# Attention on one core: the exponential of 15 of 256 score units computed on VectorE and GpSimd

## The chip, the cores and the metric

The kernel runs on one core of a Trainium2 chip. The metric is the device time of one execution in microseconds (us). TensorE (PE in the profile) multiplies matrices, ScalarE (ACT) evaluates functions such as exp, VectorE (DVE) and GpSimd (POOL) do elementwise work, and SyncE (SP) issues most of the transfers. SBUF is the on-chip working memory and PSUM the memory that TensorE writes its results to. All of these run in parallel; each takes its own instructions in order, and waits on the others through semaphores.

## The reference

```python
def reference(q, k, v):                       # each (8, 8, 512, 64), float32
    scale = 1.0 / np.sqrt(q.shape[-1])
    scores = np.einsum('bhqd,bhkd->bhqk', q, k) * scale
    scores = scores - scores.max(axis=-1, keepdims=True)
    attn = np.exp(scores)
    attn = attn / attn.sum(axis=-1, keepdims=True)
    return np.einsum('bhqk,bhkd->bhqd', attn, v)
```

There are 64 heads of 512 queries and 512 keys, each with 64 features. The inputs are standard normal numbers, and the kernel takes the exponential of the scaled scores without subtracting the maximum.

## The kernel before, in words

Heads are taken in 32 pairs g. For a pair, q, k and v are loaded as float32 (`load`, L66, on SP's queue), six pairs ahead. GpSimd casts q and k of both heads into one float16 tile (`cast_qk`, L86 to L95, tag qk, four buffers, three pairs ahead) and v into a tile with a column of ones beside it (`cast_v`, L97 to L103, five tiles vp used in turn). TensorE transposes q and k of the pair in eight 128x128 matmuls into PSUM, and VectorE copies the result to SBUF (`transpose`, L108 to L120, tile tqk).

The score work is cut into 256 units (g, c, h): 128 keys (chunk c of 4) by 512 queries of head h. One matmul of 512 columns makes a unit's scores, keys on the partitions (`scores`, L152 to L161). Three units share one PSUM tile st of 128x1536; there are two such tiles. One ScalarE instruction takes the exponential of all three into the float16 tile pt (`softmax`, L163 to L166, eight buffers). The list `sizes` (L146) cuts the units into groups of 1, 1, 2, then 3 throughout, then 2 and 1.

For each head, `attend` (L201 to L208) multiplies the exponentials with v: 16 matmuls of 128 queries by 65 columns over the four key chunks (`weigh`, L170 to L181), into a PSUM tile o. The 65th column is the sum of the exponentials, by the column of ones. `normalise` (L183 to L193) takes its reciprocal (L187, tile rcp) and multiplies (L188, tile osb) on VectorE, both reading o from PSUM. `save` stores both heads of a pair on SP's queue (L196).

The transposes and the o tiles share one small PSUM ring: `aux` (L105, tag ps_x) has two buffers, so a tile can be written only when the tile two before it has been read out.

The order of everything is written out by hand in the main loop (L270 to L298), once per group j: `softmax(j)`, then `scores(j + 1)`, then whatever falls due for the units of group j - 1. With the first unit of a pair g come `cast_qk(g + 3)`, `cast_v(g + 2)` and the loads of pairs g + 6 (q, k) and g + 5 (v). With its third unit a transpose of g + 2 is put in the list `work`, and with the last key chunk of a head that head's `attend`. A group lets pieces of `work` go while its credit lasts:

```python
            credit = min(credit + 0.42 * n, 2.0)
            while work and (credit >= 1.0 or j > len(sizes) - 6):
                f, *a = work.popleft()
                f(*a)
                credit -= 1.0
```

So one or two such pieces are issued per group of three units. Each engine's queue follows this order: on TensorE the scores of a group stand ahead of its pieces of work; on VectorE there is a copy or a normalisation for each piece; on GpSimd there are three casts per pair; on SP there are three loads per pair and one store. The first pair (L218 to L268) and the last head (`close`, L210) have code of their own.

Of the kernel before, what the change touches and what calls it, by code (L numbers as in the profile page):

```python
# [8 lines left out]

FP32 = mybir.dt.float32  # L10
FP16 = mybir.dt.float16

EXP = mybir.ActivationFunctionType.Exp
AluOp = mybir.AluOpType


@with_exitstack
def kernel(
# [4 lines left out]
    v: bass.AP,  # L23
    out: bass.AP,
):

    nc = tc.nc
    B, H, S, D = q.shape  # L30
    P = 128
    NI = S // P
    assert NI == 4 and D == 64 and S == 512
    scale = float(D) ** -0.5
    W = D + 1

    n_pairs = (B * H) // 2
    ppb = H // 2
    UPP = 2 * NI
    last = n_pairs - 1  # L40
    units = []
    for g in range(n_pairs):
        if g in (0, last):
            first = NI - 1 if g == 0 else 0
            units += [(g, (first + c) % NI, h) for h in range(2) for c in range(NI)]
        else:
            units += [(g, c, h) for c in range(NI) for h in range(2)]
    n_units = len(units)
    G = 3
    NV = 5  # L50
    AHEAD = 6
# [4 lines left out]
    ppool = ctx.enter_context(tc.tile_pool(name="att_p", bufs=8))  # L56
# [9 lines left out]
    def load(g, names="qkv"):  # L66
        if g >= n_pairs:
            return
        for nm in names:
            r = lpool.tile([P, 2, NI * D], FP32, tag=f"{nm}32", name=f"{nm}32_{g}")  # L70
            nc.sync.dma_start(out=r, in_=rows(dict(q=q, k=k, v=v)[nm], g))
            raw[g, nm] = r

    def load_head(h, nm, eng):
        if ("head", h) not in raw:
            raw["head", h] = cpool.tile([P, 2 * NI, D], FP32, name=f"raw_0_{h}")
        lo = NI * "kq".index(nm)
        eng.dma_start(
            out=raw["head", h][:, lo : lo + NI].rearrange("p (o i) d -> p o (i d)", o=1),
            in_=rows(dict(q=q, k=k)[nm], 0, h, h + 1),  # L80
        )

    vps = [cpool.tile([P, 2, NI, W], FP16, name=f"vp{n}") for n in range(NV)]
    halves, tqk, turned = {}, {}, {}

    def cast_qk(g):  # L86
        if g >= n_pairs:
            return
        qk = xpool.tile([P, 2, NI, P], FP16, tag="qk", name=f"qk_{g}")
        for n in range(2):  # L90
            nc.gpsimd.tensor_copy(  # L91
                out=qk[:, n].rearrange("p i (h d) -> p i h d", d=D),
                in_=raw[g, "qk"[n]].rearrange("p h (i d) -> p i h d", d=D),
            )
        halves[g] = qk  # L95
# [9 lines left out]
    def aux(shape, dt, name):  # L105
        return pspool.tile(shape, dt, tag="ps_x", bufs=2, name=name)

    def transpose(g, parts=(0, 1)):  # L108
        if g >= n_pairs:
            return  # L110
        if g not in turned:
            turned[g] = xpool.tile([P, 2, S], FP16, tag="tqk", name=f"tqk_{g}")
            for h in range(2):
                tqk[g, h] = [turned[g][D * h : D * (h + 1), n] for n in range(2)]
        lo, hi = parts[0], parts[-1] + 1
        ps = aux([P, hi - lo, NI, P], FP16, f"tps_{g}_{lo}")
        for n in parts:
# [7 lines left out]
    def open_cast(h, eng, lo, hi):  # L125


        if ("x", h) not in raw:
            raw["x", h] = cpool.tile([P, N, D], FP16, name=f"x_0_{h}")
            f = cpool.tile([D, NI + 1, P], FP16, name=f"t_0_{h}")  # L130
            r = cpool.tile([D, FIRST, P], FP16, name=f"r_0_{h}")
            raw["t", h] = f, r
            keys = [r[:, c] for c in range(FIRST)] + [f[:, 0]]
            tqk[0, h] = (f[:, 1:].rearrange("d n p -> d (n p)"), keys)
        eng(out=raw["x", h][:, lo:hi], in_=raw["head", h][:, lo:hi])  # L135
# [9 lines left out]

    sizes = [1, 1, 2] + [G] * ((n_units - 7) // G) + [2, 1]  # L146
    assert sum(sizes) == n_units
    firsts = [sum(sizes[:j]) for j in range(len(sizes))]
    where = {units[f + x]: (j, x) for j, (f, s) in enumerate(zip(firsts, sizes)) for x in range(s)}
    st, pt = {}, {}  # L150

    def scores(j):  # L152
        if j >= len(sizes):
            return
        if j not in st:
            st[j] = pspool.tile([P, G, S], FP32, tag="ps_st", bufs=2, name=f"st_{j}")
        for x in range(sizes[j]):
# [2 lines left out]
            key = tk[c] if g == 0 else tk[:, c * P : (c + 1) * P]  # L160
            nc.tensor.matmul(st[j][:, x, :], key, tq, start=True, stop=True)  # L161

    def softmax(j):  # L163
        n = sizes[j]
        pt[j] = ppool.tile([P, G, S], FP16, tag="pt", name=f"pt_{j}")
        nc.scalar.activation(out=pt[j][:, 0:n], in_=st[j][:, 0:n], func=EXP, scale=scale)  # L166
# [2 lines left out]

    def weigh(g, h, o, chunks, blocks=range(NI)):  # L170
        for c in chunks:
            j, x = where[g, c, h]
            for i in blocks:
                nc.tensor.matmul(  # L174
                    o[:, i, :],
                    pt[j][:, x, i * P : (i + 1) * P],
                    vps[g % NV][:, h, c, :],
                    start=(c == 0 and i == blocks[0]),
                    stop=(c == NI - 1),
                    skip_group_check=True,  # L180
                )  # L181
# [36 lines left out]
    with tc.manual_schedule():  # L218
        load_head(0, "q", nc.sync)
        load_head(0, "k", nc.scalar)  # L220
        load_head(1, "q", nc.sync)
        load_head(1, "k", nc.scalar)
        blank = cpool.tile([P, P], FP16, name="blank")
        nc.vector.memset(blank, 0.0)
        small = cpool.tile([P, 1], FP32, name="small")
        nc.vector.memset(small, 0.0)  # L226
        nc.scalar.activation(out=small, in_=small, func=EXP, scale=scale)  # L227
        ident16 = cpool.tile([P, P], FP16, name="ident16")
        make_identity(nc, ident16)
        load(1, "qk")  # L230
        load(0, "v")
        for g in range(2, AHEAD):
            load(g, "qk")
            load(g - 1, "v")
        for n in range(NV):
            nc.vector.memset(vps[n][:, :, :, D:W], 1.0)
        def busy(tile, n):
            for _ in range(n):
                nc.tensor.matmul(tile[:, G - 1, 0:P], blank, blank, start=True, stop=True)  # L239

        busy(pspool.tile([P, G, S], FP32, tag="ps_st", bufs=2, name="warm"), 24)
        A, V, Y = nc.scalar.copy, nc.vector.tensor_copy, nc.gpsimd.tensor_copy
        open_cast(0, V, 3, 6)
        open_cast(0, A, 6, 8)
        open_cast(0, A, 0, 3)
        open_cast(1, Y, 0, 3)
        a1, a2 = (aux([D, N, P], FP16, f"open_{n}") for n in range(2))
        a3 = pspool.tile([D, N, P], FP16, tag="ps_st", bufs=2, name="open_2")
        open_turn(0, 3, 6, a1)
        open_turn(0, 6, 8, a2)  # L250
        open_turn(0, 0, 3, a3)
        open_copy(0, V, 3, 6, a1)
        open_copy(0, A, 6, 8, a2)
        open_cast(1, V, 3, 8)
        open_copy(0, V, 0, 3, a3)
        st[0] = pspool.tile([P, G, S], FP32, tag="ps_st", bufs=2, name="st_0")
        busy(st[0], 4)
        scores(0)
        scores(1)
        b1, b2 = (aux([D, N, P], FP16, f"open_{n + 3}") for n in range(2))  # L260
        open_turn(1, 3, 8, b1)
        open_turn(1, 0, 3, b2)
        open_copy(1, V, 3, 8, b1)
        open_copy(1, V, 0, 3, b2)
        cast_qk(1)
        cast_v(0)
        cast_qk(2)
        cast_v(1)  # L268

        work = deque()  # L270
        credit = 0.0
        for j, n in enumerate(sizes[:-1]):
            softmax(j)
            if j > 0:
                scores(j + 1)
                if j == 2:
                    transpose(1, (0,))
                    transpose(1, (1,))
                for u in range(firsts[j - 1], firsts[j - 1] + sizes[j - 1]):
                    g, c, h = units[u]  # L280
                    r = u % UPP
                    if r == 0:
                        cast_qk(g + 3)
                        cast_v(g + 2)
                        load(g + AHEAD, "qk")
                        load(g + AHEAD - 1, "v")
                    if r == (5 if g == 0 else 2) and g + 2 < n_pairs:
                        work.append((transpose, g + 2))
                    if c == (FIRST - 1 if g == 0 else NI - 1):
                        work.append((attend, g, h))  # L290
            credit = min(credit + 0.42 * n, 2.0)
            while work and (credit >= 1.0 or j > len(sizes) - 6):
                f, *a = work.popleft()
                f(*a)
                credit -= 1.0
        while work:
            f, *a = work.popleft()
            f(*a)  # L298
        close()
# [30 lines left out]
```

The softmax here doesn't subtract the row's maximum and nothing guards it: scores larger than these inputs give would overflow.

## Time and profile before

| | us |
|---|---|
| median of the 3 runs shown | 129.53 |
| lowest and highest of them | 126.96, 129.73 |
| the profiled execution | 126.88 |
| its span, first to last instruction | 125.1 |
| ScalarE busy in the span | 117.5 |
| TensorE matmuls busy | 107.2 |
| VectorE busy | 60.7 |
| GpSimd busy | 58.9 |

The profile is of one execution. Its page gives the busy time of each engine, the span in 40 slices, the DMA queues, the chain of work that ended last, and groups of instructions: line, engine and operation, output tile <- input tiles with shapes, count | busy us, mean ns of one | idle time of the engine just before them, and what ended most of it. Timelines list start, length, engine, line and instruction. TensorE's granted clock was 0.999 of full speed. The DMA queues moved 33.81 MB at a mean of 270 GB/s.

### The profile page before, as it was taken

Reading aid. Unit: us, or ns where it says so; the run is one execution under the profiler, and the core shown is the slowest. Engines: PE = TensorE matmul, PEld = TensorE weight load, DVE = VectorE, ACT = ScalarE, POOL = GpSimd, SP = SyncE. Lnnn points to the kernel's source line nnn. Section 1 sums busy time; section 2 is a strip of 40 time slices with the busy share of each in tenths; the row PEclk is TensorE's granted clock in tenths of the full one; section 3 lists DMA queues with packets and bytes.
Section 4 is the critical chain, followed back from the end, with each engine's and each line's share of the span. In section 5 each row is a group of like instructions: output and inputs, shape, how many; then the busy total and the mean of one; then the engine's idle time right before and its main releaser. Section 6 shows DMA issues by size and latency. Waiting matters only on the chain.

```text
span 125.1 us, 3986 instructions
## 1 busy us (share of the span) xinstructions
PE 107.2 (86%) x1572; PEld 63.9 (51%) x1572; DVE 60.7 (49%) x173; ACT 117.5 (94%) x93; POOL 58.9 (47%) x101
## 2 busy tenths in 40 slices
PE   6999979889997987999798798979979898997780
PEld 6636536455464454565455265545536455554450
DVE  0344536553653745445454554645546563553450
ACT  4499999999999999999999999999999999999970
POOL 2188878576565173376347523644753753000000
PEclk9999999999999999999999999999999999999999
DMA  3999999999997699999789878989999974222222
GB/s 111 290 354 350 349 350 370 365 372 375 359 355 220 177 298 332 368 341 330 219 252 364 284 246 212 368 278 289 375 302 282 350 262 147 89 84 86 89 78 89
DMA packets 34882, 33.81 MB, mean 270 GB/s; under 512 B 2096, under 2 KB 34864, under 8 KB 34864
## 3 DMA queue, kind: packets, MB, share of 16 engines
q1 hardware_dynamic: 34576, 33.30, 82.0%
q8 instruction: 12, 0.20, 0.7%
q10 hardware_dynamic: 288, 0.26, 0.6%
q14 instruction: 6, 0.05, 0.1%
HBM read 25.17 MB, written 8.39 MB: 268 GB/s over the span
## 4 chain that ended last, share of the span: by engine, by line
ACT 74%; issue 16%; PE 4%; DMA 2%; DVE 1%
ACT pt L166 74%; DMA raw<-in_k_dram 2%; PE open L139 1%; PE st L161 1%; PE o_last L174 1%; PE o L174 0%; PE st L239 0%; DVE osb L188 0%; DVE x L135 0%; DVE rcp L187 0%
## 5 line engine op out<-in xcount | busy, mean ns | idle before, releaser
L166 ACT ACTIVATE pt<-st 128x1536 f16<-128x1536 f32 (+2 forms) x88 | 115.1, 1597 | 1.0 <-PE st L161 1.0
L161 PE MATMUL st<-tqk 64*128 64x512 f16 x248 | 49.6, 380 | 13.1 <-ACT pt L166 11.5
L174 PEld LDWEIGHTS <-pt 128*128 128x128 f16 x1024 | 33.8, 98 | 18.0 <-issue 16.2
L174 PE MATMUL o<-vp,pt 128*128 128x65 f16 x1008 | 38.4, 194 | 0.0
L91 POOL CAST qk<-q 128x512 f16<-128x512 f32 x31 | 19.1, 616 | 27.4 <-DMA q<-in_q_dram 19.6
L187 DVE RECIPROCAL rcp<-o 128x4 f32<-128x4 f32 x63 | 11.3, 180 | 38.8 <-PE o L174 38.8
L120 DVE COPY tqk<-tps 128x1024 f16<-128x1024 f16 (+1 forms) x32 | 21.5, 675 | 15.4 <-PE tps L119 15.4
L188 DVE TENSOR_TENSOR osb<-o,rcp 128x256 f32<-128x256 f32 x63 | 26.7, 425 | 2.2
L100 POOL CAST vp<-v 128x512 f16<-128x512 f32 x32 | 19.8, 619 | 10.6 <-DMA v<-in_v_dram 6.4
L161 PEld LDWEIGHTS <-tqk 64*128 64x128 f16 x248 | 11.6, 93 | 23.4 <-issue 14.8
L91 POOL CAST qk<-k 128x512 f16<-128x512 f32 x31 | 19.1, 616 | 5.6 <-DMA k<-in_k_dram 4.7
L119 PEld LDWEIGHTS <-qk 128*128 128x128 f16 x248 | 13.9, 98 | 13.1 <-issue 9.3
L119 PE MATMUL tps<-ident,qk 128*128 128x128 f16 x248 | 19.2, 220 | 0.0
L239 PE MATMUL warm<-blank 128*128 128x128 f16 x24 | 2.7, 310 | 1.0 <-DVE small L226 1.0
L239 PEld LDWEIGHTS <-blank 128*128 128x128 f16 x28 | 2.8, 142 | 1.2 <-DVE small L226 1.0
L227 ACT ACT_TABLE_LOAD x1 | 1.3, 1283 | 1.7 <-PEq L314 1.7
L161 PE MATMUL st<-t,r 64*128 64x512 f16 x6 | 2.0, 381 | 0.0
L139 PE MATMUL open<-ident,x 128*64 128x128 f16 x16 | 1.7, 268 | 0.2 <-DVE x L135 0.2
L135 DVE CAST x<-raw 128x192 f16<-128x192 f32 (+1 forms) x2 | 0.6, 284 | 2.5 <-DMA raw<-in_k_dram 2.5
L135 POOL CAST x<-raw 128x192 f16<-128x192 f32 x1 | 0.3, 344 | 3.0 <-DMA raw<-in_k_dram 3.0
L139 PEld LDWEIGHTS <-x 128*64 128x64 f16 x16 | 1.3, 138 | 0.9 <-DVE x L135 0.4
L144 DVE COPY t<-open 64x384 f16<-64x384 f16 (+1 forms) x2 | 0.8, 416 | 1.7 <-PE open L139 1.7
(20 smaller groups left out, 6.5 us busy)
## 6 DMA issues: line engine op xcount, KB each, us to landing
v<-in_v_dram SPq DMA_DIRECT2D x32, 256.0 KB, 5.6
q<-in_q_dram SPq DMA_DIRECT2D x31, 256.0 KB, 5.2
k<-in_k_dram SPq DMA_DIRECT2D x31, 256.0 KB, 5.6
out_dram<-osb SPq DMA_DIRECT2D x31, 256.0 KB, 4.8
raw<-in_k_dram ACTq DMA_DIRECT2D x2, 128.0 KB, 2.9
raw<-in_q_dram SPq DMA_DIRECT2D x2, 128.0 KB, 2.8
out_dram<-osb SPq DMA_DIRECT2D x2, 128.0 KB, 1.7
```

Of the source, the lines that this page charges most:

```text
L91: nc.gpsimd.tensor_copy(out=qk[:, n].rearrange("p i (h d) -> p i h d", d=D), in_=raw[g, "qk"[n]].rearrange("p h (i d) -> p i h d", d=D),)
L100: nc.gpsimd.tensor_copy(out=vps[g % NV][:, :, :, 0:D], in_=raw[g, "v"].rearrange("p h (i d) -> p h i d", d=D),)
L119: nc.tensor.transpose(ps[:, n - lo, i, :], halves[g][:, n, i, :], ident16)
L120: nc.vector.tensor_copy(out=turned[g][:, lo:hi], in_=ps)
L139: nc.tensor.transpose(ps[:, i - lo, :], raw["x", h][:, i, :], ident16)
L161: nc.tensor.matmul(st[j][:, x, :], key, tq, start=True, stop=True)
L166: nc.scalar.activation(out=pt[j][:, 0:n], in_=st[j][:, 0:n], func=EXP, scale=scale)
L174: nc.tensor.matmul(o[:, i, :], pt[j][:, x, i * P : (i + 1) * P], vps[g % NV][:, h, c, :], start=(c == 0 and i == blocks[0]), stop=(c == NI ...
L187: nc.vector.reciprocal(out=rcp[:, lo:hi], in_=o[:, lo:hi, D:W])
L188: nc.vector.tensor_tensor(out=o_sb[g][:, h, lo:hi], in0=o[:, lo:hi, 0:D], in1=rcp[:, lo:hi].broadcast_to([P, hi - lo, D]), op=AluOp.mult,)
L227: nc.scalar.activation(out=small, in_=small, func=EXP, scale=scale)
L239: nc.tensor.matmul(tile[:, G - 1, 0:P], blank, blank, start=True, stop=True)
```

## The change

Fifteen units, (g, 0, 0) for g = 2, 4, ..., 30, are taken out of the list `units` and so out of ScalarE's groups: 241 units remain, in five groups of three fewer. Each of the fifteen gets its scores by a matmul of its own into the small PSUM ring (tile sa), and its exponential in eight elementwise instructions of 128x512. With y = score x scale x log2(e), VectorE writes the rounded n (16-bit integer) and f = y - n, both from PSUM. GpSimd makes e, the integer n x 2^23 + 1008520192, which read as a float32 is 2^n times the leading coefficient of the quartic; and b = (f + P2) x f in two instructions. VectorE then makes a = (f + P1) x f, a = (a + Q1) x e, and pa = (b + Q2) x a in float16, each from two SBUF tensors. `weigh` takes pa in place of the slice of pt.

The pieces are a generator. It is started with the first unit of the pair before the one that it serves (g odd), and one step is issued per group, ahead of that group's pieces of work: the matmul, n, f and the three GpSimd instructions; then a; then the second a; then pa. The GpSimd instructions stand behind the casts issued with the same unit. In VectorE's queue, two pairs now hold, in order: n, f, a normalisation, a, a copy, a, two normalisations, pa, a copy, a normalisation. In GpSimd's queue, two pairs hold six casts, then e, b and b times f. The temporary tiles have two buffers each. No transfer is added or taken away.

```diff
+P1, Q1 = 0.7988556027412415, 13.09467887878418
+P2, Q2 = 5.044106960296631, 7.979714393615723
+LEAD_BITS = 1008520192
+LOG2E = 1.4426950408889634
...
+    aside = [(g, 0, 0) for g in range(2, last, 2)]
+    units = [u for u in units if u not in aside]
     n_units = len(units)
+    first_of = {g: next(n for n, u in enumerate(units) if u[0] == g) for g in range(n_pairs)}
...
+    apart = {}
+
+    def exp_aside(g):
+
+        _, c, h = unit = next(u for u in aside if u[0] == g)
+        tq, tk = tqk[g, h]
+
+        def tmp(nm, dt=FP32):
+            return ppool.tile([P, S], dt, tag=nm, bufs=2, name=f"{nm}_{g}")
+
+        n, e, f, a, b = tmp("n", I16), tmp("e", I32), tmp("f"), tmp("a"), tmp("b")
+        out16 = tmp("pa", FP16)
+
+        def split():
+            s = aux([P, S], FP32, f"sa_{g}")
+            nc.tensor.matmul(s, tk[:, c * P : (c + 1) * P], tq, start=True, stop=True)
+            nc.vector.tensor_scalar(
+                out=n, in0=s, scalar1=scale * LOG2E, scalar2=-126.0, op0=AluOp.mult, op1=AluOp.max
+            )
+            nc.vector.scalar_tensor_tensor(
+                out=f, in0=s, scalar=scale * LOG2E, in1=n, op0=AluOp.mult, op1=AluOp.subtract
+            )
+            nc.gpsimd.tensor_scalar(
+                out=e,
+                in0=n,
+                scalar1=float(1 << 23),
+                scalar2=float(LEAD_BITS),
+                op0=AluOp.mult,
+                op1=AluOp.add,
+            )
+            nc.gpsimd.tensor_scalar(
+                out=b, in0=f, scalar1=1.0, scalar2=P2, op0=AluOp.mult, op1=AluOp.add
+            )
+            nc.gpsimd.tensor_tensor(out=b, in0=b, in1=f, op=AluOp.mult)
+
+        def step(o, x, k, y, op1=AluOp.mult):
+            nc.vector.scalar_tensor_tensor(
+                out=o, in0=x, scalar=k, in1=y, op0=AluOp.add, op1=op1
+            )
+
+        yield split()
+        yield step(a, f, P1, f)
+        yield step(a, a, Q1, e.bitcast(FP32))
+        step(out16, b, Q2, a)
+        apart[unit] = out16
+        yield
...
         for c in chunks:
-            j, x = where[g, c, h]
+            p = apart.get((g, c, h))
+            if p is None:
+                j, x = where[g, c, h]
+                p = pt[j][:, x]
             for i in blocks:
                 nc.tensor.matmul(
                     o[:, i, :],
-                    pt[j][:, x, i * P : (i + 1) * P],
+                    p[:, i * P : (i + 1) * P],
...
-        work = deque()
+        work, steps = deque(), deque()
...
-                    r = u % UPP
+                    r = u - first_of[g]
                     if r == 0:
+                        if any(a[0] == g + 1 for a in aside):
+                            steps.append(exp_aside(g + 1))
                         cast_qk(g + 3)
...
+            while steps and next(steps[0], 1) == 1:
+                steps.popleft()
             credit = min(credit + 0.42 * n, 2.0)
```

More of the change, by code (lines that the diff above doesn't have):

```diff
@@ L11 @@
 FP16 = mybir.dt.float16
+I32 = mybir.dt.int32
+I16 = mybir.dt.int16
 EXP = mybir.ActivationFunctionType.Exp
 AluOp = mybir.AluOpType
+P1, Q1 = 0.7988556027412415, 13.09467887878418
+P2, Q2 = 5.044106960296631, 7.979714393615723
+LEAD_BITS = 1008520192
+LOG2E = 1.4426950408889634
 @with_exitstack
```

## The prediction

> **What bounds the kernel now.** I read the page's busy times and groups first, then the chain that ended last, then the table of waits, and last the timelines of PE, DVE and POOL. The page:
>
> ```profile
> PE 107.2 (86%) x1572; PEld 63.9 (51%) x1572; DVE 60.7 (49%) x173; ACT 117.5 (94%) x93; POOL 58.9 (47%) x101
> ...
> ACT 74%; issue 16%; PE 4%; DMA 2%; DVE 1%
> ...
> L166 ACT ACTIVATE pt<-st 128x1536 f16<-128x1536 f32 (+2 forms) x88 | 115.1, 1597 | 1.0 <-PE st L161 1.0
> ...
> L91 POOL CAST qk<-q 128x512 f16<-128x512 f32 x31 | 19.1, 616 | 27.4 <-DMA q<-in_q_dram 19.6
> ```
>
> The L166 line is the kernel: 88 exponentials, 115.1 us busy, 1.0 us idle before them in all. ScalarE never waits once it has started, and the windows of 10 us from 10 to 120 show it busy 10.00 in each. "issue" in the chain is the overlap of one exponential with the next, not idleness. By form, 83 of the 88 are of 1536 columns and hold 111.7 us, so one costs 111.7 / 83 = 1.346 us from start to start (its record of 1.642 overlaps its neighbour's).
>
> Two pairs of heads, 16 units, are what repeats: 16 / 3 x 1.346 = **7.18 us**. The other engines have to do their part of two pairs in that time. The timelines give each one's pace, start to start. PE:
>
> ```profile
> 62.29 0.60 PE L161 MATMUL st<-tqk 64*128 64x512 f16 x3
> 62.83 0.62 PE L119 MATMUL tps<-ident,qk 128*128 128x128 f16 x8
> 63.38 0.60 PE L161 MATMUL st<-tqk 64*128 64x512 f16 x3
> ```
>
> Three scores take 0.54, a transpose 0.55, and the 32 weighing matmuls of two heads (61.20 to 62.29) 1.09. Per two pairs: 16 x 0.18 + 2 x 0.55 + 4 x 0.545 = 6.16 us. DVE, of which two normalisations and a copy:
>
> ```profile
> 15.11 0.42 DVE L188 TENSOR_TENSOR osb<-o,rcp 128x256 f32<-128x256 f32 x1
> 15.45 0.17 DVE L187 RECIPROCAL rcp<-o 128x4 f32<-128x4 f32 x1
> 15.65 0.42 DVE L188 TENSOR_TENSOR osb<-o,rcp 128x256 f32<-128x256 f32 x1
> 16.47 0.69 DVE L120 COPY tqk<-tps 128x1024 f16<-128x1024 f16 x1 [0.39 <-PE tps L119]
> ```
>
> A normalisation is 0.22 + 0.34 = 0.56 us, a copy 0.69 on record and about 0.61 to the next instruction (the multiply, on record 0.42, lets the next start after 0.34). Per two pairs: 4 x 0.56 + 2 x 0.61 = 3.46 us. POOL, six casts:
>
> ```profile
> 32.41 0.62 POOL L91 CAST qk<-q 128x512 f16<-128x512 f32 x1 [1.42 <-PE o L174]
> 33.06 0.62 POOL L91 CAST qk<-k 128x512 f16<-128x512 f32 x1
> 33.87 0.62 POOL L100 CAST vp<-v 128x512 f16<-128x512 f32 x1 [0.19 <-DMA v<-in_v_dram]
> 34.61 0.62 POOL L91 CAST qk<-q 128x512 f16<-128x512 f32 x1
> ```
>
> q, k and v of a pair take 34.61 - 32.41 = 2.20 us, six casts 4.40; 3.70 of it is recorded work, 0.70 gaps. POOL often waits for data, and all its casts are done by 103 us.
>
> [...] no VectorE line there has two SBUF inputs (L188 and L120 read PSUM), and the casts are 616 to 617 ns without exception[...]
>
> **The change, part by part.**
>
> *ScalarE.* 15 units leave it: five exponentials of 1536 fewer, 5 x 1.346 = 6.7 us. Two pairs with an aside unit are 15 / 3 x 1.346 = 6.73 us. With nothing else late that is the end: 126.88 - 6.7 = 120.1 for the profiled execution.
>
> *TensorE.* The same 256 score matmuls; the aside one goes to the small PSUM ring (tag ps_x, two buffers). PE needs 6.16 of 6.73 us, at no cost. But each ring buffer is taken again two tiles later, so the transpose behind the aside scores waits until DVE has read them twice (1.4 us). By hand this makes that transpose some 0.35 us late, less than the slack between a score and its exponential: nothing on the path while DVE keeps up.
>
> *VectorE*, five new instructions per two pairs, of 512 elements. n and f read PSUM[...]; f waits for n, so 0.73 + 0.61 = 1.34 us. Three steps (a, a, pa) from SBUF[...]. Together 3.1, and with the old 3.46: 6.57 of 6.73 us. DVE fits with hardly any room. In its order each step stands ahead of the group's copy or normalisations: what is queued behind a waiting step is tqk (PE's next scores wait for it) and the rcp/osb that free the ring (PE's next attend, then the store and the loads behind it in SP's queue).
>
> *GpSimd*, three new ones: e and b, one input each, at least the cast's 0.62[...]. 4.40 + 0.62 + 0.62 + 1.11 = **6.75 us**: already all of the 6.73. And they tie POOL to the present: e needs n, which needs this pair's scores, so POOL can no longer run ahead. The second DVE step waits for e, two groups (2.7 us) after n; the third for b times f. If POOL is late with six casts it is late with e, DVE stands, PE's ring fills, and ScalarE waits.
>
> *The two together.* The three steps all have two SBUF inputs. [...] Bounds: 0 (no contention, or always in gaps) and 3 x 0.69 = 2.1 (whole records). POOL's two pairs become 6.75 + 1.15 = **7.9 us** against 7.18 before. There are 15 such stretches: 15 x (7.90 - 7.18) = +10.8 us. ScalarE's saving is inside this difference: the two-pair period is set by POOL now.
>
> *SP.* No DMA is added. The loads follow the stores in the same queue and shift with them; at 268 GB/s over the span against 370 in the best slices, they are not the bound.
>
> Sum: 126.88 + 10.8 = **137.7 us**, against the profiled execution's 126.88 (span 125.1 and 1.8 around it). The runs shown have a median of 129.53 and reach from 126.96 to 129.73; the profiled one stands at their low end.
>
> **The rivals.**
>
> *A, not slower: steps and POOL run side by side.* Then 6.75 (POOL) and 6.57 (DVE) stand beside ScalarE's 6.73 and the period is about 6.8: 126.88 - 15 x 0.38 = 121.2 us. It decides if one step holds POOL up by less than (7.18 - 6.75) / 3 = 0.14 us. For it: nothing in the trace of before shows a contention, and 0.15 us gaps do exist. Against: [...] POOL is nearly always in a read, so a step seldom finds it free.
>
> *B: no full exclusion, but the balance is spent on waits.* A step waits for the rest of a cast (half of 0.62, three times, 0.9 us) while POOL loses little: DVE becomes 6.57 + 0.5 to 0.9 = 7.1 to 7.5[...]. The period is around 7.2, the time 125 to 131, no change. For it: DVE's 6.57 leaves 0.16. Against: it needs contention to strike one side only.
>
> *C: the PSUM ring sets the pace.* The aside scores hold a buffer for 1.4 us and PE stops before the transpose and the attend after it. In the waits of before, PE waits for DVE nearly nowhere (0.3 us for tqk), so there is slack; I worked out 0.35 us per stretch at most outside the slack: 15 x 0.35 = 5 us given back, 125 to 126. That the aside units might not leave ScalarE isn't a rival: the unit list shrinks to 241, and the exponentials with it.
>
> **How the numbers follow.** POOL and steps exclude each other: 0.52 (own range 129 to 147: period 7.35 to 8.5). A: 0.26 (119.5 to 123.5). B and C: 0.22 (123.5 to 131). About 2% either way is what a measurement of this kernel can tell from no change. Faster by over 2%: A and a part of C, 0.29; within: the rest of B and C and the lightest contention, 0.18; slower: 0.53. The range takes in A without its lowest end: 120.5 to 146.
>
> **What would show it.** Right: DVE a and pa lines whose mean is well over 691 ns or that idle on POOL; casts no longer all 616; ScalarE idle over 10 us, ended by PE st; POOL busy or blocked through the middle of the span. Wrong: steps at 600 to 700 ns beside running casts, the casts unchanged, and ScalarE still without a gap: then A holds. A multiply near 0.6 us on POOL would also pull the time towards no change.

## The result, and the profile after

The change makes the kernel slower: 1.034 times the time before (95% interval 1.024 to 1.044). Its four runs are 130.92, 131.74, 138.06 and 139.86 us; the two long ones (granted clock 0.985 and 0.981, against 0.993 and 1.000 in the short ones) are disturbed executions of the same kernel: ratios and times here leave such runs out, and from the profiles of gated, left_out, third_one_input and quad, which caught one, only the rhythm in the middle of the span is read. The forecast was 137.7 us. The profiled execution took 131.74 us, its span 130.0, against 126.88 and 125.1 before.

The page of the changed kernel, its busy times, its chain and four groups (after the count: busy us, mean ns of one, idle time ahead and what ended it):

```profile
PE 108.4 (83%) x1572; PEld 63.4 (49%) x1572; DVE 110.3 (85%) x248; ACT 114.9 (88%) x88; POOL 109.9 (85%) x146
...
DMA 45%; POOL 31%; DVE 10%; issue 5%; PE 4%; SPq 1%; POOLq 0%
...
L226 ACT ACTIVATE pt<-st 128x1536 f16<-128x1536 f32 (+2 forms) x83 | 112.5, 1408 | 8.7 <-PE st L174 6.6
...
L209 POOL TENSOR_TENSOR b<-b,f 128x512 f32<-128x512 f32 x15 | 25.8, 1721 | 1.2
L104 POOL CAST qk<-k 128x512 f16<-128x512 f32 x31 | 25.8, 833 | 0.5
...
L104 POOL CAST qk<-q 128x512 f16<-128x512 f32 x31 | 18.9, 608 | 1.6 <-DMA q<-in_q_dram 1.2
```

Five exponentials are gone and 83 remain, but ScalarE, which had waited 1.0 us in all, now waits 8.7 us, mostly for scores. VectorE and GpSimd went from 61 and 59 us busy to 110 each, what they wait inside an instruction included: of the qk casts, which had all taken 616 ns, q is as before (608) and k has a mean of 833. The chain names transfers for 45%, and that is misleading: GpSimd waits for q and v 1.9 us in all, and in the middle of the span starts each instruction as the last one ends. The q cast at 62.88 below is an example: the chain puts a transfer that landed at 62.53 ahead of it, but it starts as the multiply before it ends.

ScalarE's timeline shows the new rhythm (start, length, instruction, and the idle time before it):

```profile
33.04 7.04 ACT L226 ACTIVATE pt<-st 128x1536 f16<-128x1536 f32 x5 [0.34 <-PE st L174]
40.41 7.04 ACT L226 ACTIVATE pt<-st 128x1536 f16<-128x1536 f32 x5 [0.34 <-PE st L174]
```

Five exponentials and one gap are 7.37 us. From 25.66 to 121.59 there are 13 such stretches, 95.93 / 13 = 7.38 us each, against 7.18 for the same two pairs before and 6.73 that ScalarE would need. The gap and the slower pace together cost 13 x 0.65 = 8.4 us; at the start, ahead of 25.66, four more gaps add 2.6. From this the 6.7 us saved are taken off: 8.4 + 2.6 - 6.7 = 4.3 of the 4.9 us by which the span grew.

One stretch on GpSimd and VectorE:

```profile
60.15 0.93 POOL L206 TENSOR_SCALAR b<-f 128x512 f32<-128x512 f32 x1
61.16 1.77 POOL L209 TENSOR_TENSOR b<-b,f 128x512 f32<-128x512 f32 x1
62.88 0.60 POOL L104 CAST qk<-q 128x512 f16<-128x512 f32 x1
63.43 1.07 POOL L104 CAST qk<-k 128x512 f16<-128x512 f32 x1
64.45 0.61 POOL L113 CAST vp<-v 128x512 f16<-128x512 f32 x1
65.01 0.61 POOL L104 CAST qk<-q 128x512 f16<-128x512 f32 x1
```

```profile
59.87 0.74 DVE L212 SCALAR_TENSOR_TENSOR a<-f 128x512 f32<-128x512 f32 x1
...
61.13 0.68 DVE L212 SCALAR_TENSOR_TENSOR a<-a,e 128x512 f32<-128x512 f32 x1
...
62.97 1.06 DVE L212 SCALAR_TENSOR_TENSOR pa<-b,a 128x512 f16<-128x512 f32 x1
```

Read them against each other. The multiply on GpSimd starts 0.03 us behind the second step and takes 1.77 us; the k cast stands behind pa, which ends at 64.03, and is over only at 64.50; b overlaps the first step. And pa, which starts while a q cast runs, takes 1.06 us where the second step took 0.68. Each time the later one waits the earlier one out, nearly to its end: b takes 0.31 us more than in one_input below, the multiply 0.50, the k cast 0.46, and pa 0.38 more than the second step. Casts that meet no step follow each other at 0.56 us.

### The profile page after: what moved, and what is told of

Same layout as the page of the kernel before. It is cut to its first block, busy times and chain, and to the rows that moved or that the text cites. A ratio compares the mean times of both kernels' runs of the same rounds, so it can differ in the third digit from the quotient of the medians.

```text
span 130.0 us, 4097 instructions
## 1 busy us (share of the span) xinstructions
PE 108.4 (83%) x1572; PEld 63.4 (49%) x1572; DVE 110.3 (85%) x248; ACT 114.9 (88%) x88; POOL 109.9 (85%) x146
## 4 chain that ended last, share of the span: by engine, by line
DMA 45%; POOL 31%; DVE 10%; issue 5%; PE 4%; SPq 1%; POOLq 0%
DMA v<-in_v_dram 36%; POOL qk L104 18%; POOL b L209 5%; DMA q<-in_q_dram 5%; DMA k<-in_k_dram 5%; POOL vp L113 4%; PE o L237 3%; DVE pa L212 3%; DVE osb L251 3%; POOL b L206 2%; DVE f L195 2%; DVE n L192 1%; POOL e L198 1%; DVE rcp L250 1%; SPq L84 1%
## 5 line engine op out<-in xcount | busy, mean ns | idle before, releaser
L209 POOL TENSOR_TENSOR b<-b,f 128x512 f32<-128x512 f32 x15 | 25.8, 1721 | 1.2
L104 POOL CAST qk<-k 128x512 f16<-128x512 f32 x31 | 25.8, 833 | 0.5
L212 DVE SCALAR_TENSOR_TENSOR pa<-b,a 128x512 f16<-128x512 f32 x15 | 15.6, 1041 | 1.5 <-POOL b L209 0.8
L206 POOL TENSOR_SCALAR b<-f 128x512 f32<-128x512 f32 x15 | 13.9, 927 | 1.2
L212 DVE SCALAR_TENSOR_TENSOR a<-a,e 128x512 f32<-128x512 f32 x15 | 10.6, 709 | 1.2 <-POOL e L198 1.2
L237 PE MATMUL o<-vp,pa 128*128 128x65 f16 x60 | 4.4, 196 | 8.1 <-DVE pa L212 8.1
L212 DVE SCALAR_TENSOR_TENSOR a<-f 128x512 f32<-128x512 f32 x15 | 11.0, 736 | 0.0
L195 DVE SCALAR_TENSOR_TENSOR f<-sa,n 128x512 f32<-128x512 f32 x15 | 10.4, 692 | 0.5
L192 DVE TENSOR_SCALAR n<-sa 128x512 int16<-128x512 f32 x15 | 10.4, 692 | 0.5 <-PE sa L191 0.5
L198 POOL TENSOR_SCALAR e<-n 128x512 int32<-128x512 int16 x15 | 9.3, 617 | 1.7 <-DVE n L192 0.5
```

The lines of the kernel that those rows point to most:

```text
L104: nc.gpsimd.tensor_copy(out=qk[:, n].rearrange("p i (h d) -> p i h d", d=D), in_=raw[g, "qk"[n]].rearrange("p h (i d) -> p i h d", d=D),)
L195: nc.vector.scalar_tensor_tensor(out=f, in0=s, scalar=scale * LOG2E, in1=n, op0=AluOp.mult, op1=AluOp.subtract)
L206: nc.gpsimd.tensor_scalar(out=b, in0=f, scalar1=1.0, scalar2=P2, op0=AluOp.mult, op1=AluOp.add)
L209: nc.gpsimd.tensor_tensor(out=b, in0=b, in1=f, op=AluOp.mult)
L212: nc.vector.scalar_tensor_tensor(out=o, in0=x, scalar=k, in1=y, op0=AluOp.add, op1=op1)
L237: nc.tensor.matmul(o[:, i, :], p[:, i * P : (i + 1) * P], vps[g % NV][:, h, c, :], start=(c == 0 and i == blocks[0]), stop=(c == NI - 1), ...
```

## The experiments

My theory after the result: GpSimd is full and sets the 7.38 us, because the three steps shut it out. The rival: VectorE, just as full, sets it by its own work.

**one_input.** The 15 units get a constant; the steps keep their waits and their length but read one SBUF tensor.

```diff
-        yield step(a, f, P1, f)
-        yield step(a, a, Q1, e.bitcast(FP32))
-        step(out16, b, Q2, a)
+        yield top(a, 0, f)                      # nc.vector.tensor_reduce, max, into one column
+        yield top(a, 1, e.bitcast(FP32))
+        top(out16, 0, b)                        # out16: a tile filled once
```

> The three VectorE steps become maxima over one SBUF tensor each (f, then e, then b, in place of a, a, pa), so that each still waits for the same GpSimd result but has a single SBUF input; the 15 units get a constant in place of their exponential. Theory (POOL is the bound, and steps with two SBUF inputs shut it out for about 1.4 us per two pairs): POOL's blocked time goes, b and b times f fall from 0.93 and 1.77 to about 0.62 and 1.15 us, the k cast from 1.07 to 0.61, POOL's two pairs from 7.38 to about 6.0 us, and ScalarE or DVE sets about 6.8: 15 x 0.58 = 9 us less than the changed kernel, 122 us. Rival (DVE's own instruction time is the bound): period and time stay, 130 to 132 us.

Measured: ratio 0.970 (0.964 to 0.976), 122.4 us in the profiled execution. The groups by form, and ScalarE's timeline:

```profile
L210 POOL TENSOR_TENSOR b<-b,f 128x512 f32<-128x512 f32 x15 | 19.1, 1272 | 1.3
L104 POOL CAST qk<-k 128x512 f16<-128x512 f32 x31 | 19.0, 614 | 0.5
...
L213 DVE TENSOR_REDUCE flat<-b 128x1 f16<-128x512 f32 x15 | 10.2, 679 | 0.3 <-POOL b L210 0.3
```

```profile
24.22 92.47 ACT L232 ACTIVATE pt<-st 128x1536 f16<-128x1536 f32 x69 [0.28 <-PE st L174]
```

The same GpSimd instructions, beside as many VectorE instructions of the same 0.68 us, take 1.27 us in place of 1.72 and 0.61 in place of 0.83, and ScalarE runs 69 exponentials without a gap that the timeline lists. The exclusion of a two-input step and the GpSimd instruction that it meets is shown: with it the change loses 3.4%, without it the same amount of work gains 3.0%. The PSUM ring is as in the change, so the ring was not what held it. The maxima also write one column in place of a whole tile, but that is not the reason: in the change f writes a whole tile too, from one PSUM and one SBUF input, and takes its 692 ns at 58.71, beside a v cast that takes 0.61 at 58.75.

TensorE is the link to ScalarE: one attend of each stretch takes pa, and later scores stand behind that attend in TensorE's queue. Its first matmuls wait 8.1 us in all in the change and 0.6 in one_input:

```profile
L237 PE MATMUL o<-vp,pa 128*128 128x65 f16 x60 | 4.4, 196 | 8.1 <-DVE pa L212 8.1
```

```profile
L243 PE MATMUL o<-vp,flat 128*128 128x65 f16 x60 | 4.4, 196 | 0.6 <-DVE flat L213 0.6
```

**no_b, no_recip, pool_more.** Which engine is full for good? GpSimd relieved (the 15 units get another polynomial), VectorE relieved (the output is not normalised), GpSimd loaded more.

```diff
# no_b
-            nc.gpsimd.tensor_scalar(out=b, in0=f, scalar1=1.0, scalar2=P2, ...)
-            nc.gpsimd.tensor_tensor(out=b, in0=b, in1=f, op=AluOp.mult)
...
-        step(out16, b, Q2, a)
+        step(out16, f, Q2, a)
# no_recip
-        nc.vector.reciprocal(out=rcp[:, lo:hi], in_=o[:, lo:hi, D:W])
# pool_more
+            nc.gpsimd.tensor_copy(out=tmp("extra", FP16), in_=f)
```

> GpSimd's two instructions for b are left out and pa takes f in place of b (the 15 units get another polynomial). VectorE's five instructions and their two-input reads stay. Theory (POOL is the bound): POOL's two pairs fall from 7.38 to about 5.4 us, DVE with waits for casts sets 6.8 to 7.1: 124 to 127 us. Rival (DVE is the bound by its own time): only the wait of pa for b goes, 0.16 us per two pairs: 129 us.

> The reciprocals are left out and the multiply takes ones (the output is not normalised): 64 VectorE instructions fewer, 0.2 us each from start to start, so 0.8 us per two pairs, with GpSimd's work and the two-input steps as in the changed kernel. Theory (POOL is the bound): the period stays 7.3 to 7.4, the time within 1.5 us of the changed kernel's 131.3. Rival (DVE is the bound): period 6.7 to 6.8, time 122 to 123 us.

> One more GpSimd cast of 128x512 per two pairs, of f, with its result unused. Theory (POOL is the bound): 0.56 to 0.7 us more per two pairs, period 7.95 to 8.1, time 131.3 + 8 to 10 = 140 us. Rival (DVE is the bound and POOL has room): no more than 2 us longer.

Measured: no_b 133.9 us, 1.057 (1.052 to 1.063); no_recip 132.2 us, 1.043 (1.034 to 1.051); pool_more 140.5 us, 1.111 (1.107 to 1.115). no_recip refutes the rival: 0.8 us less work on VectorE shortens nothing (stretches of 7.34), and pool_more came as my theory has it. But no_b refutes my theory as well, and lies outside both ranges: 1.9 us less work on GpSimd makes the kernel *slower*, with stretches of 7.71. Its groups, and pieces of GpSimd's timeline:

```profile
L208 DVE SCALAR_TENSOR_TENSOR pa<-f,a 128x512 f16<-128x512 f32 x15 | 15.4, 1025 | 0.0
...
L208 DVE SCALAR_TENSOR_TENSOR a<-a,e 128x512 f32<-128x512 f32 x15 | 15.0, 1001 | 0.6 <-POOL e L198 0.6
...
L198 POOL TENSOR_SCALAR e<-n 128x512 int32<-128x512 int16 x15 | 9.3, 617 | 35.6 <-PE o L233 31.6 <-DVE n L192 3.9
```

```profile
60.16 0.61 POOL L104 CAST qk<-q 128x512 f16<-128x512 f32 x1
...
63.87 0.61 POOL L113 CAST vp<-v 128x512 f16<-128x512 f32 x1
67.19 0.62 POOL L198 TENSOR_SCALAR e<-n 128x512 int32<-128x512 int16 x1 [2.71 <-PE o L233]
```

GpSimd idles 35.6 us ahead of e, and yet two steps take 1.0 us in place of 0.68. Freed of b, it starts the casts right behind e, from 60.16 to 64.48, just where all three steps fall (they start at 60.51, 61.84 and 63.91), and then has nothing to do while VectorE runs a copy, a normalisation, n and f, which it would not disturb (in gated below six casts of 0.61 and 0.62 us run beside these, and n and f take 692 ns as in the change). So it is not only how much GpSimd does, but when.

**deferred and gated.** This tests just that. A cubic, (f + P1) f + Q1 times f + R, needs e alone from GpSimd, with as many VectorE instructions. The six casts of two pairs are put behind pa, one pair further ahead, with a fifth qk buffer; in gated one GpSimd instruction of one column, which reads pa, holds them back.

```diff
-        step(out16, b, Q2, a)
+        step(out16, f, R, a)
+        nc.gpsimd.tensor_copy(out=gate, in_=out16[:, 0:1])   # gated only
+        while pend:
+            casts(pend.pop(0))                               # cast_qk(g + 4), cast_v(g + 2)
```

> A cubic in place of the quartic: GpSimd makes e alone, and pa = (f + R) x a, as many instructions on each engine as in no_b. The six casts of two pairs stand behind the pa step in program order, one pair further ahead, but nothing holds them back: GpSimd starts them as soon as e is done. This is the control for the next run. If the placement of the casts in time is what matters, they still fall beside the steps: period 7.4 to 7.7 and 129 to 134 us, like no_b. If GpSimd's amount of work is what matters, it was already small in no_b, and the result is the same.

> As deferred, with one more GpSimd instruction of one column that reads pa, ahead of the six casts: they can start only when the last two-input step is done, and run beside the copy, the normalisations, n and f, which have one SBUF input or none. Theory (a step and a reading GpSimd instruction exclude each other, and what counts is how they meet in time): VectorE's steps fall to 0.68 to 0.75 us, the period to 6.75 to 7.0, ScalarE almost without gaps, 122 to 125 us. Rival (VectorE has too much to do, 6.5 us of its own and the round through TensorE for pa): the period stays near 7.4 to 7.7, 129 to 134 us. Second rival: the casts come too late and TensorE's transposes wait for them, above 130 us.

Measured: deferred 135.1 us, 1.067 (1.055 to 1.078), stretches of 7.71; gated 126.5 us, 0.999 (0.997 to 1.000), stretches of 7.10. VectorE's timeline in deferred, then VectorE's and GpSimd's in gated:

```profile
62.59 1.05 DVE L208 SCALAR_TENSOR_TENSOR a<-a,e 128x512 f32<-128x512 f32 x1
...
64.66 1.11 DVE L208 SCALAR_TENSOR_TENSOR pa<-f,a 128x512 f16<-128x512 f32 x1
```

```profile
59.31 0.97 DVE L209 SCALAR_TENSOR_TENSOR a<-f 128x512 f32<-128x512 f32 x1
...
60.81 0.68 DVE L209 SCALAR_TENSOR_TENSOR a<-a,e 128x512 f32<-128x512 f32 x1
...
62.50 0.68 DVE L209 SCALAR_TENSOR_TENSOR pa<-f,a 128x512 f16<-128x512 f32 x1
```

```profile
63.32 0.19 POOL L217 COPY gate<-pa 128x1 f16<-128x1 f16 x1 [2.56 <-DVE pa L209]
...
66.23 0.62 POOL L113 CAST vp<-v 128x512 f16<-128x512 f32 x1
```

One more instruction on GpSimd, and the kernel is 6% faster than in deferred, since two of the three steps now meet no cast. The two kernels differ in nothing else, so the placement of the casts in time is shown as a cause. The time is above what I expected (122 to 125): the first step (the next one starts at 66.41) still waits 0.30 us for the end of the sixth cast.

**two_gates, quad_gated, quad.** In two_gates two casts stand behind a gate on the second step and four behind pa. The other two use a quadratic, so one step fewer: quad_gated with gated's casts and gate, quad with the casts where the change has them, four qk buffers and no gate.

> As gated (cubic, 15 units), but the six casts are split: two run behind the second step, beside the two normalisations, and four behind pa. In gated the first step still waits 0.30 us for the sixth cast; here the casts should be over before it. Theory (exclusion, and its placement in time): period 6.85 to 7.0 in place of 7.10, 122.5 to 125 us. Rival (VectorE's own work and the round through TensorE set 7.1 whatever the casts do): 126 to 127 us, as gated.

> A quadratic (its relative error on the 15 units is 0.0017, the cubic's 0.00007), so one two-input step and one VectorE instruction fewer per two pairs: a = (f + P) x f, pa = (a + Q) x e, with the casts held back behind pa. VectorE has 0.6 us less to do than in gated, and POOL's casts have longer to run without a step beside them. Theory: ScalarE's pace of 6.73 is reached, 120.5 to 122.5 us. If the PSUM ring holds TensorE up (aside scores read twice by VectorE), the period stays above 6.9: 124 us or more.

> The quadratic of quad_gated with the casts where the change leaves them, right behind e and so beside the two steps. VectorE's own work is the same as in quad_gated (122.95 us, ScalarE without a gap), GpSimd's too but for the one-column gate. Theory (placement in time): each of the two steps waits 0.2 to 0.4 us for a cast, period 6.9 to 7.2, 124.5 to 128 us. Rival (the smaller amount of work alone made quad_gated fast): within 1 us of quad_gated.

Measured: two_gates 125.2 us, 0.987 (0.981 to 0.994), stretches of 6.99; pa waits 0.20. quad_gated 122.6 us, 0.969 (0.959 to 0.978), just above what I expected; quad 129.5 us, 1.021 (1.018 to 1.023), worse than I expected, with stretches of 7.30. The step pa in quad_gated, then in quad:

```profile
L208 DVE SCALAR_TENSOR_TENSOR pa<-a,e 128x512 f16<-128x512 f32 x15 | 10.2, 682 | 0.0
```

```profile
L207 DVE SCALAR_TENSOR_TENSOR pa<-a,e 128x512 f16<-128x512 f32 x15 | 15.4, 1024 | 0.0
```

The same arithmetic gains 3.1% or loses 2.1%, by where the casts fall; the fifth buffer and the extra pair ahead differ too, but deferred had both and gained nothing from them. Of the two versions that beat the kernel before, two_gates does so by less than the 2% that counts as a change here; the cubic of two_gates has a relative error of 0.00007 on the 15 units, the quadratic 0.0017.

**left_out.** The exponential of the 15 units is left out, the scores stay.

```diff
-            nc.vector.tensor_scalar(out=n, ...)
-            ...
-            nc.gpsimd.tensor_tensor(out=b, in0=b, in1=f, op=AluOp.mult)
...
-        yield step(a, f, P1, f)
-        yield step(a, a, Q1, e.bitcast(FP32))
-        step(out16, b, Q2, a)
+        yield
+        yield
```

> The exponential of the 15 units is left out altogether (a constant stands in its place; the score matmuls stay): what five exponentials of 1536 fewer are worth when nothing takes their place. By ScalarE's pace: 5 x 1.346 = 6.7 us less than before, 120 us of 126.8; ratio 0.947. If TensorE cannot follow at 6.73 us per two pairs, less than that is gained: 122 to 124 us.

Measured: 120.0 us, 0.949 (0.939 to 0.960): the saving is real and TensorE can follow.

**every_3rd and third_one_input.** Nine units, one in every third pair; then the same with the one-input steps.

```diff
-    aside = [(g, 0, 0) for g in range(2, last, 2)]
+    aside = [(g, 0, 0) for g in range(2, 27, 3)]
```

> The change with 9 aside units, one in every third pair, in place of 15. Saving on ScalarE 3 x 1.346 = 4.0 us. The stretch of five groups with the steps still takes 7.2 to 7.4 us against ScalarE's 6.73, but a pair without steps follows in which VectorE and GpSimd catch up; ScalarE can be held back at most by what the two score tiles cannot cover, 0.3 to 0.5 us a stretch. Theory: 126.8 - 4.0 + 9 x 0.4 = 126.4 at worst, 123 at best. If the loss of the changed kernel were spread over the whole span instead (a slower ScalarE or transfers), 9 of 15 of it would show: 129 to 130 us.

> Nine aside units, one in every third pair, with the three steps as maxima over one SBUF tensor (a constant stands for the exponential of the nine), against every_3rd at 136.7. If every_3rd lost its time to the exclusion of the two-input steps and GpSimd, it goes here: 126.8 - 4.0 = 122.5 to 124 us, ScalarE without gaps. If it was the PSUM ring (another order of transposes, attends and aside scores than with every second pair), most of it stays: 128 us or more.

Measured: every_3rd 136.1 us, 1.077 (1.064 to 1.089), far outside what I expected; third_one_input 128.1 us, from a single run, too few for a ratio. So some 8 us of every_3rd are the exclusion. Nine units' share of what the exclusion cost the change (its 131.3 us against 122.9 in one_input) would be 5 us, so placement counts here too. The 4 to 6 us above the 122.5 to 124 expected are something else. TensorE's timeline in third_one_input:

```profile
68.64 0.66 PE L243 MATMUL o<-vp,pt 128*128 128x65 f16 x16
70.22 0.65 PE L243 MATMUL o<-vp,pt 128*128 128x65 f16 x16 [0.91 <-DVE f L196]
```

Here two attends follow the aside scores in one group, and the second has to wait until f has released the ring: rival C, in a stretch that every second pair never produces. ScalarE's gaps from this, 1.13 us three times, explain 3.4 of the 4 to 6 us; the rest I leave open.

## Why the prediction was wrong

The direction and the mechanism were right, the size was not: +10.8 us was forecast, +4.9 us came for the profiled execution.

*ScalarE, TensorE.* Right: left_out took 120.0 us, the sum gives 120.1, and 83 exponentials are in the trace. (Two readings of before were slightly off: v casts take up to 620 ns, and the last cast ends at 106.1 us. Nothing rests on them.)

*VectorE's own time.* Right. The 3.1 us for the five new instructions were my estimate; the trace of before has none of them. In after n and f show 692 ns, steps that meet nothing 0.68 us with 0.60 to the next. Own work of two pairs, by its timeline: 0.72 + 0.61 + 4 x 0.545 + 2 x 0.60 + 3 x 0.60 = 6.51 us (6.57 forecast). Missed: pa, TensorE's attend and its normalisation stand in one round, and VectorE waits some 0.2 us for it. In one_input, where no step is held up, the round from f to f is 67.98 - 61.19 = 6.79 us:

```profile
61.19 0.69 DVE L196 SCALAR_TENSOR_TENSOR f<-sa,n 128x512 f32<-128x512 f32 x1
...
67.98 0.69 DVE L196 SCALAR_TENSOR_TENSOR f<-sa,n 128x512 f32<-128x512 f32 x1
```

*GpSimd's own time.* This is the term that failed. I took six casts at 4.40 us, from a stretch in which they partly waited for data and for buffers; full, they follow at 0.56, and six with the step to e take 3.48. By one_input's timeline e and b are 0.70 each from start to start (0.62 forecast), the multiply 1.22. Its 1.11 in the forecast was my estimate: before has no two-input instruction on GpSimd. The sum is 6.1, not 6.75. With the measured stretch the prediction's own last line gives 15 x (7.38 - 7.18) = 3.0 us in place of 10.8; the rest of the 4.9 us lies outside the 13 even stretches, at the start above all (gaps of 0.95 and 0.94 us), for which I had no term and whose cause I did not follow.

*The exclusion.* Right in kind. That the three steps would shut GpSimd out, for 3 x 0.38 = 1.15 us, was my estimate, and the trace of before did not show it. Measured are 1.27 us: (0.93 - 0.62) + (1.77 - 1.27) + (1.07 - 0.61). 6.10 + 1.27 = 7.37. In this stretch the later of the two waits for the rest of the earlier one to within some 0.15 us: b, the multiply and the k cast lose 0.31, 0.50 and 0.46 us, where the records of the steps ahead of them have 0.46, 0.65 and 0.60 left.

*"The two-pair period is set by POOL now."* Wrong as it stands. Taking work from either engine alone did not help. I had charged the exclusion to GpSimd and put VectorE's waits into rival B, at 0.5 to 0.9; both sides are struck at once. The round of 6.8 us plus what VectorE's steps wait for GpSimd gives the stretch of seven kernels (waits: lengths of the steps less 0.68 each, in after also 0.15 us that pa waits for b):

| | steps wait, us | 6.8 + waits | measured |
|---|---|---|---|
| after | 0.59 | 7.39 | 7.38 |
| no_b, deferred | 0.92 | 7.72 | 7.71 |
| gated | 0.29 | 7.09 | 7.10 |
| two_gates | 0.20 | 7.00 | 6.99 |
| pool_more | 1.10 | 7.90 | 7.89 |
| quad | 0.49 | 7.29 | 7.30 |

The 6.8 us are not VectorE's work alone: quad_gated, with a step fewer, has 6.81, and VectorE waits 0.68 us of it for TensorE. In no_recip the sum does not hold (6.8 - 0.8 + 1.19 = 7.2 against 7.34): there GpSimd, without a gap, sets the pace. In after the table gives 7.39 and GpSimd's sum 7.37. Both are read off the same stretch, so they say where the time went; which of the two engines leads they cannot tell.

*Rivals.* A is what one_input shows (122.4 us; 121.2 worked out), had there been no exclusion. B came nearest in time, 125 to 131 beside the change's 131.3, for half of the reason. C added nothing to the loss: TensorE waits 2.8 us in all for normalisations that free the ring, in the change and in one_input alike. In third_one_input it did cost time. Of the signs named beforehand, all came but one: ScalarE idle 8.7 us, not over 10.

## What to carry to other kernels

Before work is moved to VectorE and GpSimd together, list which VectorE instructions have two SBUF inputs: beside a busy GpSimd the three of the change cost GpSimd 1.27 us of a stretch of 7.38 and VectorE 0.44, and a sum of their times one by one did not show it. Then ask what runs at that moment, not only how much there is: an engine that runs ahead freely can be made to wait, with a tiny dependent instruction (0.19 us in gated), until the other has nothing that it would disturb. Here that found room because GpSimd no longer made b (in gated it idles 2.56 us a stretch ahead of the gate instruction); with the change's own quartic the gate was not tried. And take an engine's pace from a stretch in which it is full, not from one in which it waits.

## What I had not expected of the hardware

Taking 1.9 us of work in 7.4 away from a full GpSimd slowed the kernel by 2.6 us (133.9 beside 131.3), since its casts moved under VectorE's steps. Casts of 128x512, recorded at 0.61 us, follow at 0.56 when nothing holds them, so the records of neighbours overlap. And in one_input the fp32 two-input multiply on GpSimd takes 1.22 us for 512 columns from start to start (1.27 on record); a one-input tensor_scalar with two operations has a record of 0.62, as long as a cast, also from 16-bit to 32-bit integers.
